# A two-layer encoder step on one core: the first FFN's matmuls in nine orders, the recurrent states in a pool of their own, the residual on another queue

## The chip, the cores and the metric

The kernel runs on one core of one Trainium2 chip. The metric is the device time of one execution in microseconds (us). The core has five engines that run side by side and wait for each other by semaphores: PE (TensorE, matmul), ACT (ScalarE), DVE (VectorE), POOL (GpSimd) and SP (SyncE, which here only issues DMAs). Matmul results land in PSUM, eight banks of 512 fp32 columns on 128 partitions; everything else lives in SBUF.

## The reference

One step of a small streaming encoder, for a prompt of 256 frames and a sample of 32 frames that share all weights; both are handled together as 288 columns. Layer 0 mixes with four retention heads and four gated linear attention (GLA) heads, layer 1 with 16 heads of band attention. Each layer ends in a ConvFFN, and a last RMSNorm gives the output.

```python
def conv_ffn(h, conv_buf, w_up, conv_w, conv_b, w_down):
    up = jnp.einsum('btd,df->btf', h, w_up)          # 2048 -> 2 x 5632
    g, u = jnp.split(up, 2, axis=-1)
    ...
    for w in range(CONV_W):                          # 3 taps along the frames
        gc = gc + gp[:, w:w + T] * conv_w[w]
    act = jax.nn.silu(gc) * u
    return jnp.einsum('btf,fd->btd', act, w_down), gp[:, -(CONV_W - 1):]

def trunk(x, ...):
    for l in range(DEPTH):                           # 2 layers
        h = rmsnorm(x, p['norm_mix_g'][l])
        mix, ... = ab_mixer(h, ...) if l % 2 == 0 else c_mixer(h, ...)
        x = x + mix
        f, buf = conv_ffn(rmsnorm(x, p['norm_ffn_g'][l]), ...)
        x = x + f
    return rmsnorm(x, p['norm_final_g']), ...
```

The states of both kinds of heads are inputs for the sample and outputs for prompt and sample.

## The kernel before

Everything is kept transposed: features on the partitions, the 288 frames along the columns. An fp32 product is made from three products of numbers cut to the PE's fp32r format: a weight tile w (128x128) is split by `weights` into wh (ACT casts, line 62) and wl = w - wh (DVE subtracts, line 63), and an activation into a high half xh and a low half xl that stand side by side in one tile of 576 columns. For each weight tile `both` issues wh times the first 320 columns (line 91: all 288 of xh and 32 of xl) and wh times the other 256 (line 92), and `high` issues wl times xh (line 95, 288 columns). I call these three matmuls a triple. The 32 columns of xl that land at PSUM columns 288 to 319 are added to the front by `joined` on DVE (lines 100 and 101).

`project` makes one 128-wide output: it goes through the input features in chunks of eight weight tiles (512 KB per chunk, one DMA on SP's queue, line 61; four buffers for w, three each for wh and wl), so an input projection is 2 chunks and 16 triples, and a down projection of one half of the FFN is 3 chunks and 22 triples. Its PSUM bank comes from a pool of four (`acc`).

The code is written in the order of the model and a scheduler (the tile framework) turns it into one fixed instruction order per engine; each engine then runs its list strictly in order, and so does each DMA-issuing queue. Where buffers of one pool are reused, or a pool takes the memory of a closed one, the framework puts waits in.

The places that matter below:

- `start`: `first_products` streams the inputs (`xw`: x and the first weights together, 12 DMAs on SP) and multiplies as they land; POOL prepares `lo_h`, the small gate weights. Then comes the product v0, `first_squares` (sum of squares on ACT and DVE), `norm_stat` (line 207: the sum over partitions by a matmul with ones, then 1/sqrt into R), and `second(0)`, the first half of the product v1. The other half is made in the first GLA head, around the gate matmul `first[3]([0])` (line 513), which needs R.
- `gla_head` and `ret_head` load the sample's states into tiles `gst` and `rst` of the mixers' pool `ab` (POOL's queue); at the end of the mixers the new retention states are written out from `rst` (line 832).
- `out_proj`: the pool `x` takes over `ab`'s memory. The residual x is loaded again, in pieces of two feature tiles (lines 294 and on), the first two pieces at once and the others one by one as it goes. After output tile m, DVE adds the product to x[m] (line 304), ACT scales it by the norm's gain (line 184), and the squares are summed.
- `ffn`, for each of two halves of the 5632 features: 22 pairs of input products (g and u), convolution, SiLU and product into the tiles `b`, then 16 down products that are added to x.

## Time and profile before

| what | value |
|---|---|
| median of three runs | 2655.47 us (2654.35 to 2659.1) |
| the profiled execution's own time | 2656.71 us |
| its span, from the first to the last instruction | 2654.9 us |
| PE busy | 2636.5 us, 99% |
| DVE busy / ACT busy / POOL busy | 1708.6 / 1123.6 / 228.9 us (64% / 42% / 9%) |
| mean granted PE clock | 0.997 of full speed |
| bytes moved by DMA | 448.31 MB, mean 169 GB/s |

In the profile a matmul is listed with its line, its output and inputs (buffer numbers left out), the columns, the number of such matmuls and their mean duration. Neighbouring matmuls overlap in the array, so the durations add up to more than the span; the distance from one start to the next is what a matmul costs. A bracket names the idle time ahead of an instruction and who ended it. The clock column gives the share of full speed that the PE was granted.

### The profile page before, as it was taken

The page shows a single profiled execution, that of the slowest core. Times are in us where ns is not written, and L with a number is a line of the kernel's source. Part 1 is how long each engine was busy: PE and PEld are TensorE (multiplying, and loading weights), DVE is VectorE, ACT ScalarE, POOL GpSimd, SP SyncE. Part 2 cuts the span into 40 slices and gives each one's busy share as a digit, 9 for nine tenths or more (in the row PEclk, how much of TensorE's full clock was granted, in tenths as well). Part 3 has the DMA queues.
Part 4 walks back from the last instruction along what each step waited for, and adds up shares of the span by engine and source line. Part 5 has one row for each costly group of instructions (what it writes and reads, how often), then busy time and mean ns, then how long its engine had stood idle before and what let it go on. Part 6 is the DMA issues. An engine that isn't in the chain of part 4 may idle for free.

```text
span 2654.9 us, 49383 instructions
## 1 busy us (share of the span) xinstructions
PE 2636.5 (99%) x20079; PEld 2618.0 (99%) x20079; DVE 1708.6 (64%) x3355; ACT 1123.6 (42%) x1511; POOL 228.9 (9%) x471
## 2 busy tenths in 40 slices
PE   9999999999999999999999999999999999999998
PEld 9999999999999999999999999999999999999997
DVE  8776666677775467776555555567777645777654
ACT  6554444443333333334444344444333333333443
POOL 3000001011110001110021110100111000111000
PEclk9999999999999999999999999999999999999999
DMA  6444555555555555555675565555555555555554
GB/s 231 152 132 160 161 162 168 184 166 167 168 167 162 169 171 168 167 170 163 169 213 181 177 188 167 160 168 165 169 167 170 161 168 173 167 167 168 166 169 132
DMA packets 127584, 448.31 MB, mean 169 GB/s; under 512 B 16155, under 2 KB 16475, under 8 KB 127356
## 3 DMA queue, kind: packets, MB, share of 16 engines
q1 hardware_dynamic: 119564, 424.47, 52.0%
q0 software_dynamic: 7648, 20.65, 2.5%
q8 instruction: 157, 2.57, 0.4%
q14 instruction: 71, 0.58, 0.1%
q10 hardware_dynamic: 144, 0.04, 0.0%
HBM read 434.69 MB, written 10.40 MB: 168 GB/s over the span
## 4 chain that ended last, share of the span: by engine, by line
PE 87%; issue 11%; DMA 0%; DVE 0%; POOL 0%; ACT 0%; DVEq 0%; POOLq 0%; ACTq 0%
PE acc L91 32%; PE acc L95 28%; PE acc L92 25%; PE mm L599 0%; PE mm L913 0%; PE mm L877 0%; DMA x<-in_xT 0%; DMA out_ret_out<-rst 0%; DVE y L370 0%; PE mm L876 0%; PE mm L207 0%; PE mm L914 0%; DMA gains<-in_gains 0%; PE mm L91 0%; PE mm L513 0%
## 5 line engine op out<-in xcount | busy, mean ns | idle before, releaser
L91 PE MATMUL acc<-x,wh 128*128 128x320 f32 x4464 | 1394.9, 313 | 0.3 <-DVE x L185 0.3
L62 ACT CAST wh<-w 128x1024 fp32r<-128x1024 f32 (+1 forms) x812 | 838.8, 1033 | 1288.1 <-PE acc L92 1044.7
L63 DVE TENSOR_TENSOR wl<-w,wh 128x1024 fp32r<-128x1024 f32 (+1 forms) x812 | 977.5, 1204 | 532.8 <-ACT wh L62 521.1
L95 PE MATMUL acc<-x,wl 128*128 128x288 f32 x4464 | 1298.4, 291 | 0.0
L92 PE MATMUL acc<-x,wh 128*128 128x256 f32 x4464 | 1246.5, 279 | 0.0
L91 PEld LDWEIGHTS acc<-x,wh 128*128 128x128 f32 x4464 | 838.4, 188 | 2.3 <-issue 1.1
L92 PEld LDWEIGHTS acc<-x,wh 128*128 128x128 f32 x4464 | 838.5, 188 | 0.8 <-issue 0.3
L95 PEld LDWEIGHTS acc<-x,wl 128*128 128x128 f32 x4464 | 836.9, 188 | 0.1
L91 PE MATMUL acc<-b,wh 128*128 128x320 f32 x1920 | 599.0, 312 | 1.9 <-ACT wh L62 1.9
L95 PE MATMUL acc<-b,wl 128*128 128x288 f32 x1920 | 560.3, 292 | 0.5 <-DVE wl L63 0.5
L92 PE MATMUL acc<-b,wh 128*128 128x256 f32 x1920 | 536.6, 280 | 0.0
L91 PEld LDWEIGHTS acc<-b,wh 128*128 128x128 f32 x1920 | 361.6, 188 | 2.7 <-ACT wh L62 2.4
L95 PEld LDWEIGHTS acc<-b,wl 128*128 128x128 f32 x1920 | 361.4, 188 | 1.1 <-DVE wl L63 0.8
L92 PEld LDWEIGHTS acc<-b,wh 128*128 128x128 f32 x1920 | 361.6, 188 | 0.0
L100 DVE COPY tail<-acc 128x32 f32<-128x32 f32 x376 | 72.0, 192 | 285.7 <-PE acc L95 282.9
L333 POOL COPY conv_out<-gp 128x2 f32<-128x2 f32 x88 | 100.3, 1140 | 1272.5 <-DVE gp L331 1272.5
L161 ACT CAST b<-v 128x288 fp32r<-128x288 f32 x88 | 38.1, 433 | 149.8 <-DVE v L348 149.8
L340 DVE SCALAR_TENSOR_TENSOR gc<-gp,convp,gc 128x290 f32<-128x290 f32 x176 | 91.8, 522 | 6.2
L101 DVE TENSOR_TENSOR acc<-acc,tail 128x32 f32<-128x32 f32 x376 | 74.8, 199 | 12.1
L162 DVE TENSOR_TENSOR b<-v,b 128x288 fp32r<-128x288 f32 x88 | 40.5, 460 | 44.0 <-ACT b L161 44.0
L331 DVE TENSOR_TENSOR gp<-acc,R 128x256 f32<-128x256 f32 x88 | 37.4, 425 | 9.1 <-DVE acc L101 0.5
L346 DVE TENSOR_TENSOR v<-acc,R 128x288 f32<-128x288 f32 x88 | 40.2, 457 | 3.0
(300 smaller groups left out, 1177.9 us busy)
## 6 DMA issues: line engine op xcount, KB each, us to landing
w<-in_w_ffn_up SPq DMA_DIRECT2D x352, 512.0 KB, 3.8
w<-in_w_ffn_down SPq DMA_DIRECT2D x128, 512.0 KB, 3.7
w<-in_w_in SPq DMA_DIRECT2D x108, 512.0 KB, 3.8
w<-in_w_qkv SPq DMA_DIRECT2D x96, 512.0 KB, 3.9
w<-in_w_ffn_down SPq DMA_DIRECT2D x64, 384.0 KB, 3.2
w<-in_w_out_ab SPq DMA_DIRECT2D x32, 512.0 KB, 3.8
w<-in_w_out_att SPq DMA_DIRECT2D x32, 512.0 KB, 3.7
x<-in_xT POOLq DMA_DIRECT2D x8, 288.0 KB, 5.0
```

Source lines behind the costliest of these rows:

```text
L62: nc.scalar.copy(h, w)
L63: nc.vector.tensor_tensor(l, w, h.bitcast(F32), op=ALU.subtract)
L91: nc.tensor.matmul(ps[:, :TX], lhsT=w, rhs=x[:, :TX], start=first, stop=last, skip_group_check=True)
L92: nc.tensor.matmul(ps[:, TX - T : T], lhsT=w, rhs=x[:, TX:], start=False, stop=last, skip_group_check=True)
L95: self.nc.tensor.matmul(ps[:, :T], lhsT=w, rhs=x[:, :T], start=False, stop=last, skip_group_check=True)
L100: self.nc.vector.tensor_copy(x, ps[:, T:TX])
L101: self.nc.vector.tensor_tensor(ps[:, :n], ps[:, :n], x, op=ALU.add)
L161: self.nc.scalar.copy(h, v)
L162: self.nc.vector.tensor_tensor(l, v, h.bitcast(F32), op=ALU.subtract)
L333: nc.gpsimd.tensor_copy(conv_out[:, f, 0:2], gp[:, TP : TP + 2])
L340: nc.vector.scalar_tensor_tensor(gc, gp[:, w : w + W], cw[:, w : w + 1], gc, op0=ALU.mult, op1=ALU.add)
L346: nc.vector.tensor_tensor(v, u, self.R, op=ALU.mult)
```

## The change

1. `project` takes a number `order`. It decides in which sequence the three matmuls of the eight weight tiles of a chunk are issued ("first" is line 91's matmul before, "rest" line 92's, "low" line 95's), and how the 576 columns are divided. All three matmuls per weight tile stay, with 864 columns together. Order 0 is the kernel before. 1: rest, first, low. 2: every other tile backwards. 3: in pairs of tiles. 5: all firsts of the chunk, then all rests, then all lows. 6: first, low, rest. 4: divided 304 + 272 + 288. 8: 288 + 288 + 288, which needs no `joined`. 9: 512 + 64 + 288. 7: the lows collect in a second PSUM bank, which DVE copies and adds at the end.
2. Only layer 0's FFN uses them. Of its first half's input pairs, four each take orders 1, 2, 3, 5 and 6; of its second half's, four each take 4, 7 and 8, and one takes 9; the down products take 1 and 3 in the first half (eight outputs each), 2 and 6 in the second. The other pairs keep order 0.
3. The states get a pool `states` of four tiles that lives through the whole program, outside `ab`: two tiles take the GLA states in pairs and later retention states again.
4. The residual's first two pieces are issued on SP's queue (`nc.sync`) and no longer on POOL's.
5. `norm_stat` of the start is called after `second(0)`, and the first head makes the other half of v1 before the first gate matmul.
6. Some small tiles of the attention's sample part have one buffer where they had two.

```diff
-    def project(self, src, x, nk, k0=0, chunks=None, part=None, ps=None):
+    def project(self, src, x, nk, k0=0, chunks=None, part=None, ps=None, order=0):
...
+        n_first = {4: 304, 8: T, 9: 512}.get(order, TX)
+        lows = self.acc() if order == 7 else ps
...
-            for j in range(n):
+            for step, j in self.steps(order, n, c == chunks[0]):
+                at = x[c + j]
                 first, last = c == chunks[0] and j == 0, c == chunks[-1] and j == n - 1
-                self.both(ps, h[:, j, :], x[c + j], first)
-                self.high(ps, l[:, j, :], x[c + j], last)
+                if step == "low":
+                    self.high(lows, l[:, j, :], at, last, first and order == 7)
+                else:
+                    self.both(ps, h[:, j, :], at, first, last and order == 7, n_first, step)
+        if order == 7:
+            self.nc.vector.tensor_copy(lows[:, T : T + 1], lows[:, :1])
+            low = self.side.tile([P, T], F32, name="lows", tag="lows", bufs=1)
+            self.nc.vector.tensor_copy(low, lows[:, :T])
+            self.nc.vector.tensor_tensor(ps[:, :T], ps[:, :T], low, op=ALU.add)
...
+    def steps(self, order, n, begins):
+        a, b, l = "first", "rest", "low"
+        if order == 3:
+            pairs = [range(j, min(j + 2, n)) for j in range(0, n, 2)]
+            return [(s, j) for p in pairs for s in (a, b, l) for j in p]
+        if order == 5:
+            return [(s, j) for s in (a, b, l) for j in range(n)]
+        of = {1: (b, a, l), 6: (a, l, b)}.get(order, (a, b, l))
+        out = []
+        for j in range(n):
+            turned = order == 2 and j % 2 == 1
+            mine = (a,) + tuple(s for s in of if s != a) if begins and j == 0 else (l, b, a) if turned else of
+            out += [(s, j) for s in mine]
+        return out
...
+        self.stp = ctx.enter_context(self.tc.tile_pool(name="states", bufs=GRP))
...
-        self.norm_stat()
         v1 = self.mm()
         second = lambda part: self.project(w[VB + 1], self.xx, KD, chunks=(0, WCH), part=part, ps=v1)
         second(0)
+        self.norm_stat()
...
-            piece(0, 2)
-            piece(2, 2)
+            piece(0, 2, nc.sync)
+            piece(2, 2, nc.sync)
...
+        of = ((1, 2, 3, 5, 6), (4, 7, 8, 9))[half]
+        at = f // 4
+        n = 1 if at < len(of) and of[at] == 9 else 4
+        return of[at] if layer == 0 and at < len(of) and f % 4 < n else 0
...
+        v1 = first[4](1) if first else self.input_product(w[VB + 2 * hd + 1])
         if first:
             first[3]([0])
-        v1 = first[4](1) if first else self.input_product(w[VB + 2 * hd + 1])
...
-        st = pool.tile([P, 256], F32, name="gst", tag="gst", bufs=GRP)
-        nc.gpsimd.dma_start(st, a["state_gla"][hd])
-        sts.append(st)
+        if hd % 2 == 0:
+            st = self.stp.tile([P, 512], F32, name="st", tag="st")
+            sts += [st[:, :256], st[:, 256:]]
+        nc.gpsimd.dma_start(sts[hd], a["state_gla"][hd])
```

How this moves instructions is seen in three places. At the head of the program, POOL before had only the gate weights to prepare (`lo_h` from the landed `xw`):

```order
L274 MEMSET lo_h 128x16x96
L131 CAST lo_h<-xw 128x16
L132 ISA
L132 TENSOR_TENSOR lo_h<-xw,lo_h 128x16
L131 CAST lo_h<-xw 128x16 x7
L132 TENSOR_TENSOR lo_h<-xw,lo_h 128x16 x7
L131 CAST lo_h<-xw 128x2x16
```

Now the state tiles `st` depend on nothing, and on POOL their loads stand there too:

```order
L308 MEMSET lo_h 128x16x96
L611 DMA st<-in_state_gla 128x256 x3
L163 CAST lo_h<-xw 128x16
L611 DMA st<-in_state_gla 128x256
L164 ISA
L164 TENSOR_TENSOR lo_h<-xw,lo_h 128x16
L163 CAST lo_h<-xw 128x16 x7
L163 CAST lo_h<-xw 128x2x16
L164 TENSOR_TENSOR lo_h<-xw,lo_h 128x16 x7
L781 DMA st<-in_state_ret 128x512
```

Six state loads have moved from the mixers to the first instructions of POOL's list, and the cast of the ninth and tenth gate tiles has gone ahead of seven subtractions.

At the start's norm, this is DVE's list before, from the low weights of the next product to the gate input `lo`:

```order
L63 TENSOR_TENSOR wl<-w,wh 128x1024
L505 MEMSET lo 33x288
L171 TENSOR_SCALAR rv<-mm 128x288
L173 TENSOR_TENSOR rs<-rs,rv 128x288
L174 SCALAR_TENSOR_TENSOR R<-rs,ry 128x288
L506 TENSOR_TENSOR lo<-acc,R 32x288
```

And this is DVE's list there after:

```order
L63 TENSOR_TENSOR wl<-w,wh 128x1024
L547 MEMSET lo 33x288
L63 TENSOR_TENSOR wl<-w,wh 128x1024
L203 TENSOR_SCALAR rv<-mm 128x288
L205 TENSOR_TENSOR rs<-rs,rv 128x288
L206 SCALAR_TENSOR_TENSOR R<-rs,ry 128x288
L132 COPY tail<-mm 128x32
L548 TENSOR_TENSOR lo<-acc,R 32x288
```

One more subtraction of weights now stands ahead of the norm's first step (its cast has moved ahead of the norm on ACT likewise), and the tail of v1 ahead of `lo`.

At the output projection, POOL before had the first residual pieces right behind the retention states' stores:

```order
L788 DMA out_ret_out<-so 128x512 x2
L832 DMA out_ret_out<-rst 128x512 x4
L294 DMA x<-in_xT 128x576 x2
L548 DMA convp<-in_convp 128x176
L548 DMA hist<-in_hist 128x88
```

SP's list after has them among the weights of the output projection:

```order
L61 DMA w<-in_w_in 128x1024 x108
L61 DMA w<-in_w_out_ab 128x1024 x10
L328 DMA x<-in_xT 128x576 x2
L61 DMA w<-in_w_out_ab 128x1024 x22
L61 DMA w<-in_w_ffn_up 128x1024 x88
```

The two pieces have left POOL's list and stand behind the tenth chunk of output weights, and what they wait for is no longer the stores of the states, whose tiles lie outside the memory that x takes.

More of the change, by code (lines that the diff above doesn't have):

```diff
@@ L94, in high @@
[L94 to L101 removed]
+        if step != "rest":
+            nc.tensor.matmul(ps[:, :n], lhsT=w, rhs=x[:, :n], start=first, stop=last, skip_group_check=True)
@@ L354, in ffn @@
             for m in range(KD):
[L355 removed]
+                ps = self.project(down[m], bb, HALF, half * HALF, order=((1, 3), (2, 6))[half][m // 8] if layer == 0 else 0)
                 nc.vector.tensor_tensor(self.x[m], self.x[m], ps, op=ALU.add)
```

57 lines of the change are left out of this document (31 added, 26 removed).

## The prediction

> **What bounds the kernel now.** I read the page's busy times first, then the waits of PE, then the order in time around each wait.
>
> ```profile
> span 2654.9 us, 49383 instructions
> PE 2636.5 (99%) x20079; PEld 2618.0 (99%) x20079; DVE 1708.6 (64%) x3355; ACT 1123.6 (42%) x1511; POOL 228.9 (9%) x471
> ```
>
> PE is the bound from end to end, so the time changes in two ways only: a triple gets dearer or cheaper, or PE idles more or less. The waits of PE say where it idles:
>
> ```profile
> PE mm L207 <- issue: 1.9, 1, 1.9
> PE acc L91 <- ACT wh L62: 1.9, 1, 1.9
> PE acc L95 <- DVE wl L63: 0.5, 1, 0.5
> ```
>
> The first is the start's norm, the other two belong to the output projection of layer 0. The table of stretches gives the price of a triple where nothing is waited for, in layer 0's FFN (columns: stretch, length, then PE, PEld, DVE, ACT, POOL busy with their instructions, clock, DMA):
>
> ```profile
> 600.00:800.00 200.00, 200.00 (x1528) 200.00 (x1527) 141.26 (x269) 77.61 (x95) 24.94 (x48) 1.00 0.54 168
> ```
>
> 1528 matmuls in 200 us are 0.131 us each, 0.3927 us per triple. DVE is busy for 71% there, ACT for 39%; neither holds PE up.
>
> **The residual on SP's queue, its memory free of the states.** PE's order in time at the output projection:
>
> ```profile
> 453.29 0.31 PE L91 MATMUL acc<-b,wh 128*128 128x320 f32 x1
> ...
> 455.75 0.55 PE L91 MATMUL acc<-b,wh 128*128 128x320 f32 x1 [1.90 <-ACT wh L62]
> 456.09 0.42 PE L92 MATMUL acc<-b,wh 128*128 128x256 f32 x1
> 457.00 0.61 PE L95 MATMUL acc<-b,wl 128*128 128x288 f32 x1 [0.50 <-DVE wl L63]
> 457.41 0.47 PE L91 MATMUL acc<-b,wh 128*128 128x320 f32 x1
> ...
> 458.13 0.47 PE L91 MATMUL acc<-b,wh 128*128 128x320 f32 x1
> ...
> 462.97 0.31 PE L91 MATMUL acc<-b,wh 128*128 128x320 f32 x1
> ```
>
> and the stretches beside it:
>
> ```profile
> 458.00:460.00 2.00, 2.00 (x10) 2.00 (x10) 1.93 (x5) 0.69 (x2) 0.00 (x0) 0.50 0.79 267
> 464.00:466.00 2.00, 2.00 (x18) 2.00 (x17) 0.89 (x2) 0.17 (x1) 0.00 (x0) 1.00 1.03 387
> ```
>
> From 453.29 to 462.97 PE does ten triples in 9.68 us; at 0.3927 they take 3.93, so 5.75 us are lost here. Only 3.3 of them are waits (two triples from 453.29 to 457.41, 4.12 us less 0.79); in the rest the granted clock is 0.50 and a triple takes 0.72 us. The reader sees that a wait of PE costs more than itself. Why did ACT come late with its weights? The chain of waits (start, length, what):
>
> ```profile
> 441.74 4.27 DMA out_ret_out<-rst
> 446.79 0.53 POOL x L294
> 447.32 5.75 DMA x<-in_xT
> ```
>
> and ACT's order in time:
>
> ```profile
> 444.32 1.05 ACT L62 CAST wh<-w 128x1024 fp32r<-128x1024 f32 x1 [2.06 <-PE acc L92]
> 453.13 0.54 ACT L184 ACTIVATE x<-x,gains 128x288 fp32r<-128x288 f32 x1 [7.76 <-DMA x<-in_xT]
> 454.66 1.03 ACT L62 CAST wh<-w 128x1024 fp32r<-128x1024 f32 x1
> ```
>
> POOL holds the residual's DMA until the states are stored out of the memory it will fill; ACT, strictly in order, waits 7.76 us for it, and the next cast of weights stands behind. After the change the load waits for SP's tenth chunk of output weights instead:
>
> ```profile
> 439.08 0.33 SPq L61 DMA_DIRECT2D w<-in_w_out_ab  x1
> ```
>
> which lands about 4.5 us after its issue (the DMA issues of that stretch):
>
> ```profile
> w<-in_w_out_ab SPq DMA_DIRECT2D x3, 512.0 KB, 4.5
> ```
>
> It is issued at about 439.5 and, beside the stores and two weight chunks, lands by 444 to 446, which is when ACT has finished its last early cast. ACT then has some 7 us in hand against 453.13. Queued behind it on SP is the eleventh chunk, whose buffer has to come free first, so the wait of 0.4 us or so holds nothing up. I take the whole 5.75 us as a gain; below it is bounded by nothing more to save, above by no gain at all if the load still waits. What is late next: nothing within 7 us on ACT, so the cover is thick.
>
> By the Trainium skill, page "TensorE: Matmul & The Clock Gate", Part 1, the clock halves only after an idle window of about 3.4 us; by that rule the idle times here (1.9 and 0.5 us) would not have halved it, the gain would be 3.3 us and the sum below 2.4 us higher. The trace shows the half clock after them, and the trace decides.
>
> **The states in their own pool.** Four GLA loads of 128 KB now go out at once on POOL, in the stretch from 2 to 14 us in which the start's input stream runs. DMA queues and issues there (the last two lines are those of the first 40 us):
>
> ```profile
> DMA packets 1883, 4.59 MB, mean 382 GB/s; under 512 B 329, under 2 KB 363, under 8 KB 1883
> q1 hardware_dynamic: 1739, 4.54, 99.9%
> xw<-in_x_first SPq DMA_DIRECT2D x8, 280.0 KB, 4.3
> gst<-in_state_gla POOLq DMA_DIRECT2D x4, 128.0 KB, 3.2
> ```
>
> The 16 DMA engines are full (99.9%), and one feature tile of 280 KB takes 0.75 us at 382 GB/s. PE needs 0.79 us for it (two outputs, two triples each 0.395 us, below), so it follows the stream with almost no slack. 524 KB more at 382 GB/s are 1.37 us; I take +1.3 us, between 0 (the added loads yield) and 1.7 (the gate subtractions on POOL that now wait for a later landing hold PE up too). The two retention loads come when PE is 1.7 us behind the stream or more: nothing.
>
> **The start's norm behind second(0).** PE, ACT and DVE in order of time:
>
> ```profile
> 28.34 0.29 PE L95 MATMUL acc<-x,wl 128*128 128x288 f32 x1
> 30.54 0.72 PE L207 MATMUL mm<-xw,ones 128*128 128x288 f32 x2 [1.91 <-issue]
> 31.30 0.50 ACT L170 ACTIVATE ry<-mm,ones 128x288 f32<-128x288 f32 x1 [1.72 <-PE mm L207]
> 34.92 0.29 PE L95 MATMUL mm<-x,wl 128*128 128x288 f32 x1
> 35.22 0.72 PE L513 MATMUL mm<-lo,w 33*128 33x288 f32 x2
> 43.39 2.35 DVE L63 TENSOR_TENSOR wl<-w,wh 128x1024 fp32r<-128x1024 f32 x2
> 44.63 0.31 PE L91 MATMUL acc<-x,wh 128*128 128x320 f32 x1
> ```
>
> The 1.91 us in front of L207, and 0.17 more before L513 (0.30 from start to start where 0.13 is usual), vanish. But from the norm's first step on ACT to the gate matmul L513 it takes 3.92 us (31.30 to 35.22), which before lay beside v1's products. Now ACT has one more cast ahead of that step, whose buffer is free only when PE has done second(0). Worked through with the start 1.3 us later: second(0) ends at 32.95, cast and norm step begin at 34.05, the gate matmul could run at about 38.1; PE is through with v1 at 36.7 and waits 1.4 us. Behind the gate the chain goes on to the low weights of the second gate product, which before were ready at 44.6 (43.39 plus half of 2.35) for a product that began at 44.63: no slack. The shifted chain delivers them about 0.9 us late. So 2.1 us are saved and 2.3 come back: +0.2, with ends of -1.2 (ACT's cast does no harm) and +1.0.
>
> **The orders.** 1760 triples change: 33 pairs of 32 triples and 32 down products of 22. The trace holds one other neighbourhood, the first products, where two outputs alternate, with a low after a low and a bank change:
>
> ```profile
> 21.14 0.30 PE L91 MATMUL acc<-x,wh 128*128 128x320 f32 x1
> ...
> 21.66 0.43 PE L95 MATMUL acc<-x,wl 128*128 128x288 f32 x2
> 21.93 0.30 PE L91 MATMUL acc<-x,lo_h 128*128 128x320 f32 x1
> ```
>
> Two triples in 0.79 us, 0.395 each: 2.3 ns above the steady ones. If all 1760 paid that, it is +4.0 us; nothing excludes as much gain, so the ends are -4 and +4. I take 0: the columns stay 864, each of the three still loads its own weights, and the neighbourhood hardly matters.
>
> Order 9 is priced apart: its 64-column matmul must also load 128x128 weights. The nearest row is that of the GLA scores, with 64 columns and new weights for each:
>
> ```profile
> 51.36 0.89 PE L599 MATMUL mm<-qk 128*128 128x64 f32 x7
> L599 PE MATMUL mm<-qk 128*128 128x64 f32 x112 | 14.6, 265 | 0.0
> ```
>
> Seven starts in 0.89 us less one duration of 0.265 are 0.104 us apart, while in proportion to 0.3927 us for 864 columns 64 would cost 0.029 to 0.036. That is 0.07 us for each of 32 triples: +2.2 us, with ends 0 and +2.6.
>
> Order 7 adds three DVE instructions per product, about 1.07 us by the row of a 288-column PSUM operation, 0.46 us, for two of them:
>
> ```profile
> L346 DVE TENSOR_TENSOR v<-acc,R 128x288 f32<-128x288 f32 x88 | 40.2, 457 | 3.0
> ```
>
> A pair lasts 12.6 us, in which DVE is busy for 8.9 (71%) and then 11.0 us. Both chunks of the next product are already split when these instructions begin, so PE has 6.3 us of cover; the fourth bank is freed about 3.3 us after g ends and needed after 6.3. Without that cover PE would wait some 3 us per pair. Cost: 0. Order 8's missing joins and the single attention buffers cost and bring nothing, DVE not being waited for there.
>
> **Sum.** -5.75 + 1.3 + 0.2 + 0 + 2.2 = -2.05 us against the profiled execution's 2656.71 us, that is 2654.7. The median shown is 2655.47, 1.2 below that execution, so I predict 2653.4 for the median. About 0.2% (5.3 us) is what a measurement of this kernel tells from no change.
>
> **Rivals.**
> - The residual still comes late. Its wait list also holds older DMAs of POOL and PE's last state matmuls; if one lands after 448, ACT blocks as before. The sum is then +3.7: 2659.2 us. Against it stand the 7 us of slack. Chance 0.08. The Trainium skill, page "Trainium Kernel Development and Optimization", section "Key Constraints", says that all queues run on the same 16 DMA engines and another queue only saves issue time; by this rule the move by itself brings nothing, and the gain rests on the changed wait alone.
> - The orders cost more than the first products show (slower). Every changed neighbourhood pays 5 ns per triple: 1760 x 5 ns = 8.8 us, 2662.2 us. It decides for slower from 4.2 ns (7.4 us over 1760). For it: the alternating triples are dearer by 2.3 ns. Chance 0.10.
> - Order 7 makes PE wait for a bank, 3.2 us for each of four pairs, 13 us: 2666 us. Chance 0.04.
> - The orders gain: 4 ns per triple, for instance because the same weights are no longer loaded twice running (orders 5 and 6) or the 320-column matmul (313 ns against 291 for 288) loses its surcharge. -7 us, 2646.4 us. Chance 0.12.
> - The early state loads cost nothing at the start: 2651.9 us. Chance 0.16.
>
> **Numbers.** The forecast, 2653.4, has a chance of 0.50. Faster by over 0.2% (below 2650.2): most of the gaining orders, a third of the free loads, a little of the forecast: 0.20. Slower (above 2660.8): most of the dear orders, order 7, some of the late residual and the forecast's edge: 0.15. Within: 0.65. The range 2647 to 2661 leaves out about 0.18: half of the gaining and most of the dear orders, and order 7.
>
> **What would show it.** Right: near 450 us no wait of ACT's gain for the residual, clock 1.00 throughout, triples of 0.39 us; in the first 12 us feature tiles that start over 0.79 us apart; a PE wait of 1 to 2 us at the gate matmul in place of that at L207, and another of about 1 us at the second gate product; 0.39 us per triple in all orders but 9, and about 0.46 in 9. Wrong: a half clock in the output projection, PE waits in the second half's input pairs four to seven, or triples that differ by 4 ns or more from 0.3927.

## The result: 0.25% slower

| | before | changed |
|---|---|---|
| median of 7 runs each, us | 2655.47 (2654.35 to 2659.14) | 2663.63 (2662.03 to 2664.81) |
| ratio, 95% interval | 1 | 1.0025 [1.0015, 1.0035] |
| profiled execution, us | 2656.71 | 2663.31 |
| its span, mean granted clock | 2654.9, 0.997 | 2661.5, 0.998 |

The forecast was 2653.4 us, with 2647 to 2661 as range; the time lies above both. The medians differ by 8.2 us (the interval goes from 4.0 to 9.3), the two profiled executions by 6.6; the account below is that of the profiled executions. The page of the changed kernel opens with these lines:

```profile
span 2661.5 us, 49416 instructions
PE 2644.4 (99%) x20079; PEld 2624.4 (99%) x20079; DVE 1711.4 (64%) x3363; ACT 1124.7 (42%) x1511; POOL 217.8 (8%) x469
```

PE is the bound as before, with as many matmuls, and its busy time grew by 7.9 us (2636.5 to 2644.4). So the loss is not a new wait: matmuls take longer. The waits of PE after the change (us in total, times, longest):

```profile
PE mm L555 <- issue: 1.1, 1, 1.1
PE acc L123 <- DVE wl L63: 1.1, 1, 1.1
PE acc L118 <- DVE x L217: 0.6, 2, 0.3
```

The 1.9 us for the late cast and the 1.9 us at the start's norm are gone; there is a wait at the gate matmul (now L555), one at low weights, and two at the first products, of which the kernel before had one (0.3 us). PE's list has the same number of matmuls in both kernels, so the starts of matmuls at the same place of the list can be subtracted. Cut at fixed places, that gives the whole account (us from one place to the next):

| stretch of PE's work | before | changed | difference | forecast |
|---|---|---|---|---|
| first products, first to 65th matmul | 8.68 | 10.68 | +2.00 | +1.3 |
| from there to behind the second gate product, with the norm | 34.51 | 34.88 | +0.37 | +0.2 |
| rest of the mixer, but for its last 37 us | 352.47 | 352.43 | -0.04 | 0 |
| these 37 us and the output projection of layer 0 | 137.44 | 131.72 | -5.72 | -5.75 |
| layer 0's FFN: order 9 | | | +2.57 | +2.2 |
| layer 0's FFN: the other orders | | | +7.05 | 0 |
| (FFN in all) | 831.41 | 841.03 | +9.62 | +2.2 |
| from there to the last matmul | 1273.46 | 1273.44 | -0.02 | 0 |
| sum | | | +6.2 | -2.05 |

**The output projection** went as forecast. SP's queue, ACT's order in time and two stretches of the changed kernel; the last row is the first of these stretches in the kernel before:

```profile
442.14 0.80 SPq L328 DMA_DIRECT2D x<-in_xT  x2
...
448.26 0.54 ACT L216 ACTIVATE x<-x,gains 128x288 fp32r<-128x288 f32 x1 [3.62 <-DVE x L338]
```

```profile
454.00:456.00 2.00, 2.00 (x18) 2.00 (x17) 2.00 (x5) 1.22 (x2) 0.54 (x1) 1.00 0.88 304
458.00:460.00 2.00, 2.00 (x18) 2.00 (x17) 1.36 (x4) 0.92 (x2) 0.54 (x1) 1.00 0.97 322
454.00:456.00 2.00, 0.26 (x1) 0.26 (x2) 1.95 (x7) 1.95 (x4) 0.77 (x4) 0.97 0.00 0
```

The residual is issued at 442.14, ACT's first gain no longer waits for a DMA, PE has 18 matmuls in each 2 us where it had 1 and 10 (the 10 stand in the prediction's rows), and the clock is 1.00.

**The orders.** The table of stretches, changed kernel; in this sequence: order 6, old order, order 3, order 8, order 7.

```profile
736.00:786.00 50.00, 50.00 (x377) 50.00 (x376) 34.98 (x67) 18.85 (x23) 6.23 (x12) 1.00 0.51 166
786.00:811.00 25.00, 25.00 (x193) 25.00 (x192) 17.62 (x34) 9.90 (x12) 3.07 (x6) 1.00 0.54 162
884.00:944.00 60.00, 60.00 (x456) 60.00 (x455) 28.05 (x42) 20.51 (x21) 0.00 (x0) 1.00 0.56 167
1054.00:1102.00 48.00, 48.00 (x365) 48.00 (x364) 31.58 (x55) 18.99 (x24) 1.96 (x12) 1.00 0.52 168
1004.00:1052.00 48.00, 48.00 (x368) 48.00 (x368) 40.02 (x85) 18.25 (x22) 1.78 (x11) 1.00 0.52 170
```

And the kernel before in the first and third of these stretches:

```profile
736.00:786.00 50.00, 50.00 (x384) 50.00 (x383) 35.23 (x69) 19.66 (x24) 6.23 (x12) 1.00 0.54 166
884.00:944.00 60.00, 60.00 (x460) 60.00 (x459) 28.80 (x42) 20.58 (x21) 0.00 (x0) 1.00 0.58 167
```

PE is busy all the time, at full clock, and gets 7 matmuls fewer through in 50 us, 4 fewer in 60. Nothing waits; the triples are dearer. From the start of the first triple of each group to the start of the next group, in ns per triple (393.3 in the kernel before; the first 128 of order 1, where the layer's norm lies between, are left out):

| order | 1, 6 | 2, 3, 8 | 4 | 5 | 7 | 9 |
|---|---|---|---|---|---|---|
| ns per triple | 399.3 to 400.0 | 396.7 | 397.8 | 394.1 | 393.4 | 473.5 |

Order 9 in PE's order of time:

```profile
1110.06 0.39 PE L118 MATMUL acc<-x,wh 128*128 128x512 f32 x1
1110.29 0.19 PE L120 MATMUL acc<-x,wh 128*128 128x64 f32 x1
1110.32 0.38 PE L123 MATMUL acc<-x,wl 128*128 128x288 f32 x1
1110.53 0.39 PE L118 MATMUL acc<-x,wh 128*128 128x512 f32 x1
```

From 512 to 512 it takes 0.47 us. The low product seems to start 0.03 us behind the 64 columns, but its follower starts 0.21 us later where 0.13 is usual: the missing time stands in the row behind the short matmul.

### The profile page after: what moved, and what is told of

Read it like the earlier page. It is cut to its first block, busy times and chain, and to the rows that moved or that the text cites. A ratio compares the mean times of both kernels' runs of the same rounds, so it can differ in the third digit from the quotient of the medians.

```text
span 2661.5 us, 49416 instructions
## 1 busy us (share of the span) xinstructions
PE 2644.4 (99%) x20079; PEld 2624.4 (99%) x20079; DVE 1711.4 (64%) x3363; ACT 1124.7 (42%) x1511; POOL 217.8 (8%) x469
## 3 DMA queue, kind: packets, MB, share of 16 engines
q8 instruction: 157, 2.57, 0.4%
## 4 chain that ended last, share of the span: by engine, by line
PE 98%; DVE 1%; ACT 0%; DMA 0%; issue 0%; SPq 0%; DVEq 0%
PE acc L118 35%; PE acc L123 31%; PE acc L120 28%; PE mm L642 0%; PE mm L956 0%; PE mm L920 0%; DMA xw<-in_x_first 0%; PE mm L460 0%; PE mm L829 0%; PE mm L708 0%; DVE y L412 0%; PE mm L919 0%; PE mm L671 0%; ACT wh L62 0%; PE mm L442 0%
## 5 line engine op out<-in xcount | busy, mean ns | idle before, releaser
L118 PE MATMUL acc<-x,wh 128*128 128x320 f32 (+2 forms) x4464 | 1354.9, 312 | 0.7 <-DVE x L217 0.6
L123 PE MATMUL acc<-x,wl 128*128 128x288 f32 x4464 | 1266.5, 293 | 1.1 <-DVE wl L63 1.1
L120 PE MATMUL acc<-x,wh 128*128 128x256 f32 (+2 forms) x4464 | 1219.0, 280 | 0.0
L118 PEld LDWEIGHTS acc<-x,wh 128*128 128x128 f32 x4464 | 827.0, 188 | 3.5 <-issue 1.5
L120 PEld LDWEIGHTS acc<-x,wh 128*128 128x128 f32 x4464 | 829.5, 188 | 0.8 <-issue 0.3
L118 PE MATMUL acc<-b,wh 128*128 128x320 f32 x1920 | 568.2, 311 | 0.0
L123 PE MATMUL acc<-b,wl 128*128 128x288 f32 x1920 | 533.6, 293 | 0.0
L120 PEld LDWEIGHTS acc<-b,wh 128*128 128x128 f32 x1920 | 357.8, 188 | 0.0
L118 PEld LDWEIGHTS acc<-b,wh 128*128 128x128 f32 x1920 | 350.5, 188 | 0.6 <-ACT wh L62 0.3
L132 DVE COPY tail<-acc 128x32 f32<-128x32 f32 (+1 forms) x366 | 69.7, 191 | 273.5 <-PE acc L123 258.7
L375 POOL COPY conv_out<-gp 128x2 f32<-128x2 f32 x88 | 76.6, 871 | 1282.0 <-DVE gp L373 1282.0
L133 DVE TENSOR_TENSOR acc<-acc,tail 128x32 f32<-128x32 f32 (+1 forms) x366 | 72.6, 198 | 11.5
```

Of the source, the lines that this page charges most:

```text
L118: nc.tensor.matmul(ps[:, :n], lhsT=w, rhs=x[:, :n], start=first, stop=last, skip_group_check=True)
L120: nc.tensor.matmul(ps[:, n - T : T], lhsT=w, rhs=x[:, n:], start=False, stop=last, skip_group_check=True)
L123: self.nc.tensor.matmul(ps[:, :T], lhsT=w, rhs=x[:, :T], start=first, stop=last, skip_group_check=True)
L132: self.nc.vector.tensor_copy(x, ps[:, T:end])
L133: self.nc.vector.tensor_tensor(ps[:, :n], ps[:, :n], x, op=ALU.add)
L375: nc.gpsimd.tensor_copy(conv_out[:, f, 0:2], gp[:, TP : TP + 2])
```

## The experiments

Each ratio is to the kernel before on the same chip, with its 95% interval.

**Apart: the orders, and all the rest.** Two runs split the change in two. In the first, every product goes back to the old order:

```diff
-        return of[at] if layer == 0 and at < len(of) and f % 4 < n else 0
+        return 0
...
-                ps = self.project(down[m], bb, HALF, half * HALF, order=((1, 3), (2, 6))[half][m // 8] if layer == 0 else 0)
+                ps = self.project(down[m], bb, HALF, half * HALF, order=0)
```

> The changed kernel with every product in the old order (first, rest, low; 320 and 256 columns, no order 9, no lows of their own), everything else as changed. Theory (the orders cost, the rest is as the two traces show): the FFN of layer 0 takes 831.4 us again instead of 841.0, so the run is 9.6 us below the changed kernel, 2654.0, and 1.5 us below the kernel before... worked from the shifts of the two traces: -5.72 at the output projection, +2.36 at the start, so -3.4 against before: 2652.1 us. Rival (the FFN is slower because of the other allocation of memory, not for its orders): FFN still near 840 us, total 2661 to 2663.

In the second, the orders stay, and the states, the residual's queue and the norm are as before. The first gate's new place and the single small buffers stay too:

```diff
+        self.norm_stat()
...
         second(0)
-        self.norm_stat()
...
-            piece(0, 2, nc.sync)
-            piece(2, 2, nc.sync)
+            piece(0, 2)
+            piece(2, 2)
...
+        st = pool.tile([P, 256], F32, name="gst", tag="gst", bufs=GRP)
+        nc.gpsimd.dma_start(st, a["state_gla"][hd])
...
-        st = self.stp.tile([P, 512], F32, name="st", tag="st")
...
+        st = pool.tile([P, 2, 256], F32, name="rst", tag="rst", bufs=GRP)
+        nc.gpsimd.dma_start(st, a["state_ret"][hd])
```

> The kernel before with the orders alone: states in the mixer's pool, the residual on POOL's queue, the norm behind v0 as before. Theory: +9.6 us in layer 0's FFN and nothing elsewhere, 2665.1 us; triples of 399 to 401 ns in orders 1 and 6, 396.7 in 2 and 3, 401 in 8, 454 in 9. Rival (the price comes from where the tiles lie in memory, so it goes with the states' pool): triples at 393.3 in all orders but 9, and 2657 us.

Measured: 2653.72 us, 0.9985 [0.9976, 0.9994], for the old orders; 2667.25 us, 1.0037 [1.0024, 1.0049], for the orders alone. Layer 0's FFN takes 831.41 us in the one and 841.02 in the other, to 0.01 us what it takes before and after the change. The expectation of the second missed two prices: order 8 takes 396.7 ns there, not 401, and order 9 473.5, not 454 (the next expectation uses this 454 again). The stretch of order 6, orders alone:

```profile
736.00:786.00 50.00, 50.00 (x378) 50.00 (x377) 34.19 (x67) 18.51 (x22) 6.75 (x12) 1.00 0.48 159
```

So the orders carry the whole loss, 9.6 us, in either layout of the memory, and without them the change would be a gain. The rival of the other allocation falls.

**What in an order costs.** A menu varies one thing at a time in the triples of the input products, 64 triples of a kind. An entry holds the weights (h: the high ones in all three), the sequence of first, rest and low (0, 1, 2), and for each its first column, its columns and its PSUM column:

```diff
+ MENU = [('', (0, 1, 2), [(0, 320, 0), (320, 256, 32), (0, 288, 0)]),
+  ('', (0, 2, 1), [(0, 320, 0), (320, 256, 32), (0, 288, 0)]),
+  ('h', (0, 1, 2), [(0, 320, 0), (320, 256, 32), (0, 288, 0)]),
...
+  nc.tensor.matmul(out[:, po : po + n_], lhsT=(l if s == 2 and key != "h" else h)[:, j, :], rhs=at[:, xo : xo + n_], ...)
```

> A menu for measuring, not a version: layer 0's input products take 22 kinds of triple in turn, two feature blocks (64 triples) each, all else as in the changed kernel with the old order; the products of that layer are not those of the reference, since columns, weights and places in PSUM are varied. Pairs of kinds hold the cycles first-rest-low (393 ns in the changed kernel) and first-low-rest (400 ns) against each other. Theory (the price hangs on the sizes of neighbouring matmuls alone): the 7 ns between the two cycles stay when all three take the same weights, when rest writes from PSUM column 0, when rest reads the high columns, and with all of these. Rivals: it hangs on the weights (7 ns vanish with the same weights thrice), on the PSUM columns (vanish with rest from column 0, or with low from column 32), on the columns read (vanish with rest from the high columns). For the division: 352/224, 384/192, 416/160, 448/128, 480/96 and 512/64 cost 393 as long as the smaller one covers the weight load of its follower, and from there on 0.42 ns per column less: by 453.6 ns at 64 the edge would lie near 200 columns. Three matmuls of 128 columns each then show the weight load itself: about 95 to 125 ns a piece, 285 to 375 ns per triple; three of 256 about 345.

Measured, in ns per triple from the starts of the records (trimmed mean of 56):

| | first, rest, low | first, low, rest |
|---|---|---|
| as in the kernel | 393.3 | 400.0 |
| high weights in all three | 393.3 | 400.0 |
| rest into PSUM column 0 | 393.3 | 400.0 |
| rest reads the high columns | 393.3 | 400.0 |
| all of these | 393.3 | 400.0 |
| low reads from column 32 | 400.6 | 398.1 |

The table of stretches shows it too; in this sequence: first-low-rest and first-rest-low of the same weights, then three of 256, and three of 128 columns:

```profile
558.00:582.00 24.00, 24.00 (x182) 24.00 (x181) 17.18 (x32) 9.29 (x12) 2.05 (x6) 1.00 0.52 173
583.50:607.50 24.00, 24.00 (x186) 24.00 (x185) 17.29 (x32) 9.50 (x12) 3.13 (x6) 1.00 0.52 174
951.00:971.00 20.00, 20.00 (x175) 20.00 (x174) 15.10 (x29) 8.45 (x11) 3.08 (x6) 1.00 0.59 191
995.00:1015.00 20.00, 20.00 (x180) 20.00 (x179) 16.50 (x34) 8.28 (x12) 3.12 (x6) 1.00 0.61 197
```

(The first of the four takes the low weights for its low product, the second the high ones; the rows of the table say that this changes nothing.) So the 7 ns between the cycles hang on the numbers of columns and their sequence; weights, PSUM columns and the place that rest reads fall as rivals. The last row is an exception: it was said of PSUM, but in this kind low reads from column 32, and that moves both. Three of 128 columns take 335 ns, three of 192 as well, 112 each, so that is a floor; three of 256 take 347, three of 288 400. The divisions 352/224, 384/192, 416/160, 448/128, 480/96 and 512/64 take 406, 421, 434, 448, 460 and 473 ns, 13.4 more for each 32 columns. This part of the expectation was wrong: it had put the edge near 200 columns, and the price rises at once beyond 320/256. A shorter rest saves nothing, since below 256 columns its place is held by the 112 ns, while the longer first costs its columns in full.

**How smooth it is.** The second menu takes 44 kinds: divisions with n columns in the first, the same in the other cycle (first, low, rest), and equal or mixed sizes. An entry now holds, for each matmul in its sequence, the weights, the first column read, the columns and the PSUM column:

```diff
+MENU = [[('h', 0, 288, 0), ('h', 288, 288, 0), ('l', 0, 288, 0)],
+ [('h', 0, 296, 0), ('h', 296, 280, 8), ('l', 0, 288, 0)],
...
+ [('h', 0, 296, 0), ('l', 0, 288, 0), ('h', 296, 280, 8)],
...
+ [('h', 0, 256, 0), ('h', 0, 256, 0), ('h', 0, 256, 0)],
...
```

> A second menu for measuring, not a version: the input products of both layers take 44 kinds of triple in turn, 64 triples each, so they are not those of the reference; all else as in the changed kernel with the old order. From the first menu: three of 288 take 400 ns, three of 256 345, three of 192 or 128 334 (111 each, the bound of the weight load), and only the sizes count. Theory A (each matmul takes the longer of 111 ns and its columns at 2.4 GHz plus 13.3 ns, less some ns for a matmul under about 272 columns): the divisions in the order first, rest, low fall from 400 at 288/288 to a lowest value at about 320/256 and rise by 0.42 ns per column beyond; the reversed cycle stays near 400 from 296 to 320 and meets it beyond 328. Theory B (320/256 is a point by itself, for instance since 256 columns are a whole number of something): 316, 318, 322 and 324 columns stand several ns above 320. Three equal matmuls of 256, 260, 264, 268, 272, 280 columns show which: a smooth rise (A) or a step behind 256 (B).

| columns of the first | 288 | 300 | 304 | 308 | 312 | 316 | 318 | 320 | 322 | 324 | 326 | 332 | 336 |
|---|---|---|---|---|---|---|---|---|---|---|---|---|---|
| ns per triple | 397 | 396 | 398 | 400 | 395 | 399 | 397 | 393 | 394 | 397 | 400 | 395 | 397 |

Three equal matmuls of 256, 260, 264, 268, 272, 280 and 296 columns take 347, 360, 361, 376, 370, 387 and 420. Neither theory holds as it stood: there is no smooth curve (268 columns cost more than 272, 296 more than the 416 of 304) and 320/256 isn't alone by itself, only the lowest of a rugged row; all lie between 393 and 401. The seven divisions tried in the other cycle take 395 to 400. The stretches of 312/264, 314/262 and 320/256:

```profile
660.00:684.00 24.00, 24.00 (x185) 24.00 (x184) 17.42 (x34) 9.61 (x12) 3.12 (x6) 1.00 0.51 174
686.00:710.00 24.00, 24.00 (x183) 24.00 (x182) 16.97 (x32) 9.17 (x12) 3.12 (x6) 1.00 0.49 169
762.00:786.00 24.00, 24.00 (x186) 24.00 (x185) 17.48 (x33) 9.41 (x12) 3.12 (x6) 1.00 0.49 174
```

No division or cycle tried beats the old one.

**Where a matmul reads.** The last menu shifts the first column that each matmul reads, all into PSUM column 0 with the high weights:

```diff
+MENU = [[('h', 0, 320, 0), ('h', 0, 256, 0), ('h', 0, 288, 0)],
+ [('h', 0, 320, 0), ('h', 0, 256, 0), ('h', 16, 288, 0)],
...
+ [('h', 16, 320, 0), ('h', 0, 256, 0), ('h', 0, 288, 0)],
...
+ [('h', 0, 320, 0), ('h', 16, 288, 0), ('h', 0, 256, 0)],
...
+ [('h', 0, 304, 0), ('h', 0, 272, 0), ('h', 0, 288, 0)],
...
+ [('h', 0, 304, 0), ('h', 304, 272, 0), ('h', 0, 288, 0)],
...
```

> A fourth menu for measuring, not a version: the input products of both layers take 44 kinds of triple, all with the high weights and into PSUM column 0, so they are not those of the reference; what varies is the column at which a matmul starts to read, beside a few sizes. What the menus before left open: reading the low columns from 32 instead of 0 moved 393.3 to 400.6 and 400.0 to 398.1, and three of 288 took 397 where the second read from column 288 and 400 where all read from 0. Theory A (reads that start off a multiple of 64 columns, 256 bytes, are dearer or shift the rhythm): starts at 64, 128 and 320 leave 393.3 as it is, starts at 16, 32, 48, 288 and 304 move it by 2 to 7 ns, and the divisions 304, 308, 312, 316, 324 and 332, read from 0 in all three, lie on a smooth line between 393 and 400. Theory B (it is a matter of lengths and phases alone, and the start of a read only shifts the phase): starts at 64 or 128 move it as much as those at 32, and the divisions read from 0 stay as rugged as before, 395 to 400 without order.

| ns per triple of 320, 256, 288 | 0 | 16 | 32 | 48 | 64 | 96 | 128 |
|---|---|---|---|---|---|---|---|
| low (288) reads from | 393.4 | 396.6 | 401.9 | 397.8 | 393.3 | 400.6 | 393.3 |
| first (320) reads from | | 399.7 | 393.3 | | 393.3 | | 393.3 |
| rest (256) reads from | | 395.5 | 393.3 | | 393.3 | | 393.3 |

The stretches of low from 32, low from 64, and of 304/272/288 read from 0 and with rest from column 304 (the kernel's order 4):

```profile
584.00:608.00 24.00, 24.00 (x182) 24.00 (x181) 16.98 (x32) 9.50 (x12) 3.13 (x6) 1.00 0.52 173
635.00:659.00 24.00, 24.00 (x186) 24.00 (x185) 17.41 (x33) 9.66 (x12) 3.13 (x6) 1.00 0.52 175
2014.50:2038.50 24.00, 24.00 (x185) 24.00 (x184) 17.24 (x32) 9.46 (x12) 3.13 (x6) 1.00 0.51 174
2065.00:2089.00 24.00, 24.00 (x183) 24.00 (x182) 17.10 (x32) 9.33 (x12) 3.14 (x6) 1.00 0.55 169
```

Half of theory A holds: starts at a multiple of 64 columns leave the price as it is, in every kind where they were tried, and in this cheap cycle a start at 16 raises it; at 32 it depends on the matmul. But off a multiple of 64 the price doesn't only rise. In the other cycle, 320, 288, 256, it falls from 400.0 to 393.5 when the 288 columns are read from 16, and three of 288 fall from 399.7 to 395.7 when the second is read from 16. Such a start is therefore not dear by itself: in what was tried it left or raised the price of the cheap sequence and lowered that of the dear ones. Order 4's division costs 393.3 when all three read from 0, so its 4.4 ns are the place that rest reads. The other half of theory A is wrong: 308, 316, 324 and 332 columns, all read from 0, still take 400, 400, 397 and 400. And three of 256 take 340 and 353 ns in turn from product to product; what alternates with the products was not varied. The last nanoseconds thus hang also on the column at which a read starts, which the order of instructions alone doesn't tell.

**Is it the weight load?** The third menu keeps the sizes and shrinks the weights:

```diff
+MENU = [(128, 128, 320, 256, 288),
+ (128, 128, 320, 288, 256),
+ (128, 64, 320, 256, 288),
...
+                    self.nc.tensor.matmul(ps[:cols, :n_], lhsT=h[:rows, j, :cols],
+                                     rhs=at[:rows, :n_], start=False, stop=last and last_s,
+                                     skip_group_check=True)
...
```

> A third menu for measuring, not a version: layer 0's input products in 22 kinds of triple, all from PSUM column 0 with the high weights, with fewer weight columns (64, 32) or fewer weight rows (64, 32) than 128; the products are not those of the reference. Theory A (the odd 7 ns of an order come from how the weight load lies beside the matmul ahead of it): with 64 or 32 weight columns or rows the load is shorter, three matmuls of 128 columns fall from 334 towards 200 ns, and the two cycles of 320, 256 and 288 columns come out alike. Theory B (they come from the columns streamed and their lengths, whatever the weights): 393 and 400 stay in every form, and 334 for three of 128 may fall or not. The last rows hold three of 64 columns (load bound: 334 again by A and B), and 512/64/288 with 64 weight columns, 473 ns if the bound is the load of any weights, nearer 400 if a load of half the columns takes half.

| weights, rows x columns | 320, 256, 288 | 320, 288, 256 | 3 of 288 | 3 of 128 | 512, 64, 288 |
|---|---|---|---|---|---|
| 128 x 128 | 393.3 | 400.0 | 400.0 | 335 (first menu) | 473 (first menu) |
| 128 x 64 | 395.0 | 393.2 | 395.1 | 180 | 415 |
| 128 x 32 | 393.2 | 393.0 | 390.0 | 180 | |
| 64 x 128 | 393.8 | 400.0 | 400.1 | | |

In this sequence: first-low-rest with 128 and with 64 weight columns, three of 128 with 64 weight columns (PE is busy for 11.99 of 15 us there, being ahead of DVE), 512/64/288 with 64 (415 is the price of three of its four products; in the first the clock was still half):

```profile
560.00:584.00 24.00, 24.00 (x183) 24.00 (x182) 17.08 (x32) 9.38 (x12) 2.06 (x6) 1.00 0.52 173
611.00:635.00 24.00, 24.00 (x185) 23.34 (x184) 17.02 (x32) 9.25 (x12) 3.13 (x6) 1.00 0.51 172
661.00:676.00 15.00, 11.99 (x179) 11.52 (x178) 12.96 (x27) 7.92 (x10) 1.52 (x3) 1.00 0.59 200
1283.00:1308.00 25.00, 25.00 (x179) 19.48 (x178) 14.81 (x29) 8.47 (x10) 2.94 (x5) 0.98 0.45 148
```

Theory A holds for the columns of the weights and not for their rows: with fewer weight columns the two cycles come out alike, the floor falls from 112 to at most 60 ns, and order 9's division loses 58 of its 80 ns; with half the rows nothing changes. So the 6.7 ns between the two cycles and most of order 9's price go with the columns of the weights. The load of the next weights, which goes on beside the matmul ahead of it, fits this: 256 columns hide it just so, 64 do not. Two things stay open. Fewer weight columns also mean fewer rows written to PSUM, and that was not tried apart. And no run shows why one sequence of the same sizes, or one start of a read, costs more than another when the weights have 128 columns in both. The Trainium skill, page "TensorE: Matmul & The Clock Gate", section "LDWEIGHTS (loading the stationary operand)", gives the load as the weights' columns divided by 1.2 ns, 107 ns for 128, whatever the rows; the runs agree to 5% with their 112, and in that 64 rows take as long as 128.

**Where the start's 2 us come from.** One run puts the norm back ahead of second(0), with the old orders:

```diff
+        self.norm_stat()
...
         v1 = self.mm()
...
         second(0)
-        self.norm_stat()
```

> As the run with the old order everywhere, and the start's norm back in its old place ahead of second(0). Theory by the prediction's step (the moved norm saves 2.1 us and gives 2.3 to 2.4 back): within 0.3 us of that run, 2651.8 us, with a wait of about 1.9 us at the norm's matmul and none at the gate. Rival (the move of the norm carries most of the 2.36 us at the start): 2650 us or less. Rival (the start's waits for late tiles had given the norm's chain its cover, and putting it back brings the old 1.9 us on top): 2654 us.

A second one also holds the state loads back until the norm is known:

```diff
+        nc.vector.tensor_copy(sts[hd][:, :1], self.R[:, :1])
         nc.gpsimd.dma_start(sts[hd], a["state_gla"][hd])
...
+        nc.vector.tensor_copy(st[:, :1], self.R[:, :1])
         nc.gpsimd.dma_start(st.rearrange("p (j v) -> p j v", j=2), a["state_ret"][hd])
```

> The run with the old order and the old place of the norm, and now each state load waits for a one-column copy of the norm's result on DVE, so that it goes out after 31 us instead of at 2 us. Theory (the early loads take the start's DMA engines from the input stream, 2.1 to 2.4 us): the first 15 us run as in the kernel before, the output projection keeps its 5.7 us, so 2.2 us less than that run, and -5.7 us (ratio 0.9979) against the kernel before on the same chip. Rival (the start is late for another cause, such as the lower clock of the first triples): no change against that run, ratio 0.9988. Rival (with the loads back at 34 us POOL's queue is late for something else): above it.

Measured: 2653.78 us, 0.9989 [0.998, 0.9998], and 2651.97 us, 0.9984 [0.9975, 0.9992]. These intervals overlap, so the whole times don't tell the two apart; the stretches of the traces do. The first is like the run with the norm moved (0.9985); in the traces the stretch with norm and gate takes 34.5 us with the norm ahead and 34.9 behind, so moving it costs 0.4 us. The first products take 10.91 us in the first and 9.09 in the second. Over all traces of versions they take 10.68 to 11.17 us in the four with early loads (mean 10.96) and 8.68 to 9.52 in the five without (mean 9.16): 1.8 us, so the theory's 2.1 to 2.4 were a little high, and the rival that the loads are not the cause falls. The rival of a lower clock in the first triples can be looked at too. In the changed kernel's trace a matmul of 256 columns takes 0.21 us there from its start to the next, where it takes 0.12 in the trace before (changed first), though the clock column gives 1.00:

```profile
5.59 0.41 PE L120 MATMUL acc<-x,wh 128*128 128x256 f32 x1
5.80 0.47 PE L118 MATMUL acc<-x,wh 128*128 128x320 f32 x1
```

```profile
5.46 0.28 PE L92 MATMUL acc<-x,wh 128*128 128x256 f32 x1
5.58 0.30 PE L91 MATMUL acc<-x,wh 128*128 128x320 f32 x1
```

The first eight matmuls take 2.08 us at this half pace, 1.22 before. It isn't the cause: the changed kernel in the old orders takes 1.17 us for them and still 11.17 for the first products, since PE then waits for the tiles instead. But it is part of the scatter among the traces without early loads. The changed kernel at the start, a wait of PE for the next tile, and the DMA queues and issues from 2 to 14 us:

```profile
9.00 0.39 PE L118 MATMUL acc<-x,wh 128*128 128x320 f32 x1 [0.25 <-DVE x L217]
```

```profile
q1 hardware_dynamic: 1577, 4.04, 88.3%
q0 software_dynamic: 192, 0.52, 12.2%
st<-in_state_gla POOLq DMA_DIRECT2D x4, 128.0 KB, 5.5
```

The states take 12.2% of the 16 engines there, 1.5 of the 12 us, and the inputs' share falls from 99.9 to 88.3%. With the states late, the inputs have 100.2% again:

```profile
q1 hardware_dynamic: 1674, 4.46, 100.2%
```

A small part of the 1.8 us, 0.1 to 0.5 us by the traces with early loads, goes through POOL instead. At the end of this stretch the gate matmuls follow POOL's subtractions, which now stand behind the cast of the ninth and tenth gate tiles: in the run with the old orders the eighth subtraction ends at 15.85 us and its matmul starts at 15.90. The prediction's upper end had allowed for this.

**Queue or memory.** The residual moved to another queue, and its memory lost the states. One run undoes the first alone, the other (from the kernel before) does the first alone:

```diff
-            piece(0, 2, nc.sync)
-            piece(2, 2, nc.sync)
+            piece(0, 2)
+            piece(2, 2)
```

> The run with the old order and the old place of the norm, with the residual's first two pieces on POOL's queue again; states stay in a pool of their own. Theory (the residual was late because its memory held the states until their stores had landed, not because of the queue): POOL issues the load without waiting for a store to land, ACT does not wait for it, and the 5.7 us stay gained: the same as that run, ratio 0.9988, clock 1.00 from 454 to 466 us. Rival (the queue is what matters): POOL's order puts it behind the four stores, ACT waits again, some 4 to 5.7 us come back, ratio 1.0005 to 1.001.

```diff
-            piece(0, 2)
-            piece(2, 2)
+            piece(0, 2, nc.sync)
+            piece(2, 2, nc.sync)
```

> The kernel before with one edit: the residual's first two pieces go out on SP's queue; states stay in the mixer's pool. Theory (the memory decides): SP now waits for the states' stores to land (to about 446 us), and the two weight chunks behind it wait too; the residual still lands at 450 to 452, PE still stalls, and the stall is as long or longer by the late weights: 0 to +3 us against the kernel before. Rival (the queue alone brings the gain): -5.7 us, ratio 0.9979.

Measured: 2655.54 us, 0.9997 [0.9988, 1.0006], with the memory alone; 2653.45 us, 0.9988 [0.9979, 0.9997], with the queue alone. The first also has the start's early loads and, in its trace, 1.57 us of half clock at the norm, so I go by the stretch of the output projection as cut above: 137.44 us before, 133.43 with the memory alone, 132.45 with the queue alone, 131.72 with both. The run with the orders alone has the old code there and takes 136.19, with a shorter half clock; the stall thus costs 4.5 to 5.7 us, the memory alone saves 2.8 to 4.0 of it and the queue alone 3.7 to 5.0. The chain of waits of the two, memory alone first:

```profile
446.43 0.53 POOL x L328
446.96 6.20 DMA x<-in_xT
```

```profile
442.65 4.08 DMA out_ret_out<-rst
446.93 3.21 DMA x<-in_xT
```

Both theories were too simple. With free memory POOL still issues the load behind its four stores, only without waiting for them to land, and it takes 6.2 us. On SP it still waits for a store to land, as said, but then needs 3.21 us, not 5.75, and PE's wait there is 0.5 us in all. Why it lands sooner there wasn't tried by itself and stays open. Either part takes most of the stall, also because the shorter waits (0.4 and 0.7 us with the memory alone) were not followed by the half clock in these two traces, memory alone first:

```profile
458.00:460.00 2.00, 2.00 (x17) 2.00 (x16) 2.00 (x5) 2.00 (x4) 0.54 (x1) 1.00 0.95 303
```

```profile
458.00:460.00 2.00, 2.00 (x17) 2.00 (x17) 1.93 (x5) 0.84 (x3) 0.00 (x0) 1.00 0.96 367
```

The two parts together take all of it.

**Cover for the gate.** The last run moves the first gates' matmul behind the next product, with the norm moved, states late and old orders:

```diff
-        if first:
-            first[3]([0])
...
         z = [gate(0)] if first else []
+        if first:
+            first[3]([0])
```

> The run with the states loaded late, with the norm behind second(0) as in the change, and one more move: the first gates' matmul goes behind the whole next product on PE (6.3 us of work) instead of in front of it. Theory (the moved norm saves its 2.1 us, and 2.4 come back because the chain from the norm to the gate, 3.9 us, has lost its cover): now the gate is covered too, from the norm to the third matmul behind the second gate product no wait of 1 us is left, and the run is 2 us below the one with the states late, 2650.0 us, ratio 0.9976 to its kernel before. Rival (DVE's later work, above all the scan of the gates that stands in its row, only moves the wait on to the low weights of another product): the 1.1 us wait at low weights stays, and 0.5 to 1 us at most are gained, ratio 0.998. Rival (the first GLA head now waits for its later sums): no gain, ratio 0.9984.

Measured: 2651.27 us, 0.9979 [0.997, 0.9988]. The stretch with norm and gate takes 33.72 us, where it takes 34.44 with the states late alone: 0.7 us, which is what the first rival gave (0.5 to 1), though not for its reason. The gate's wait is gone, that at the low weights too, and another one stands ahead of the next product:

```profile
37.38 0.39 PE L118 MATMUL acc<-x,wh 128*128 128x320 f32 x1 [1.18 <-DVE lo L548]
```

The product needs a PSUM bank that still holds the gate's input until DVE has multiplied it by the norm. So the norm's result has a second user that PE waits for. This version beats the kernel before by 0.2% and the changed one by 0.5%, the best of the runs; the interval of the run with the states late overlaps with it.

## Why the prediction failed, step by step

- **The orders (forecast 0, measured +7.05 us): the step that failed.** It said "the columns stay 864, each of the three still loads its own weights, and the neighbourhood hardly matters". The runs showed that the sequence of the three matmuls, their division and the column at which rest reads cost up to 6.7 ns per triple, 4.1 on the mean of 1728 triples, with PE busy throughout and wherever the states and the residual lie. The price is uneven: orders 1 and 6 carry about 3.8 of the 7.05 us, order 7 nothing. The ends of the term, -4 and +4 us, were too narrow as well: they came from the one other neighbourhood in the trace, 2.3 ns dearer per triple, and a single row doesn't bound eight other sequences. Of the rivals "the orders cost more" (5 ns per triple, 2662.2 us) came nearest, at a chance of 0.10, and the prediction's own sign of being wrong, triples that differ by 4 ns or more, is there in orders 1, 4 and 6, and on the edge in 2, 3 and 8. The row that spoke for it was there, the first products. I set the price to 0 because it could also have gone the other way; the steady 0.3927 us of one good cycle was no reason for that.
- **Order 9 (forecast +2.2, measured +2.57, end +2.6): right.** The row of the 64-column scores gave 0.104 us for a matmul with new weights; the floor measured here is 0.112.
- **The residual (forecast -5.75, measured -5.72): right in the mechanism, with some luck in the number.** The half clock is gone with the wait, but the same old code lost 1.25 us less in the run with the orders alone, and against that run the gain is 4.5 us. The prediction's sentence that the move to another queue by itself brings nothing did not hold: alone it brought 3.7 to 5.0 us.
- **The state loads (forecast +1.3, measured +2.00, +1.8 over all traces): right in kind, just outside the upper end of 1.7.** The 1.37 us were bytes by rate; in the trace the packets held the engines for 12.2% of 12 us, 1.46 us. The trace of before (8.68) was the shortest of the five without early loads; the means of the two groups differ by 1.8 us. The rival of free loads should read 2652.1 us by the prediction's own terms (2653.4 less 1.3), not 2651.9.
- **The norm (forecast +0.2, measured +0.37): right**, with the waits of 1.1 us at the gate and 1.1 us at the second gate product where 1.4 and 0.9 were said.
- **Order 7 and order 8's joins (forecast 0): right.** 393.4 ns in order 7 with DVE busy for 40.02 of 48 us; 396.7 in order 8 is the price of its division read as in the kernel (397 in the menu).
- **The sum.** With the orders' 7.05 us and the 0.7 us that the start's term lacked it would have been +5.7, within 0.5 us of the account. The other 2 us by which the medians lie apart are within what runs of the same kernel differ by (4.8 us between the lowest and the highest of the kernel before).

## What to carry to other kernels

On an engine that is busy 99% of the time, an order of instructions isn't free until a row shows that very order: where a neighbouring order in the trace already costs 0.6% more, forecast a loss and a range wider than that one row. Keep matmuls long enough to hide the load of the next weights (here 256 columns for 128 weight columns), and when you divide columns unevenly, count the short one at no less than that load. Measure a sequence together with the columns at which it reads: here starts at a multiple of 64 columns changed nothing, and others moved a triple by up to 8.5 ns, up or down. Loads that nobody needs yet should not be freed to start while the input stream fills the DMA engines: one wait on a late result got 1.8 us back.

## What the runs showed of the hardware beside that

A wait of the same length may or may not be followed by the half clock. The norm's wait at the start is 1.9 us in both of these runs with the same code ahead of it; the first is the one with the norm back, the second that with the residual on POOL:

```profile
35.00:37.00 2.00, 2.00 (x17) 2.00 (x17) 0.88 (x2) 1.32 (x4) 2.00 (x7) 1.00 0.83 257
```

```profile
35.00:37.00 2.00, 2.00 (x10) 2.00 (x10) 0.85 (x2) 1.08 (x3) 2.00 (x8) 0.50 0.81 242
```

The second lost 1.57 us by it (36.05 against 34.48 us for the stretch with norm and gate), which has nothing to do with its edit. The Trainium skill, page "TensorE: Matmul & The Clock Gate", Part 1, calls the window in which idle time is counted free-running, which fits that difference; its 3.4 us of idle time do not fit a half clock behind 1.9 us.

The clock also fell with PE busy throughout: in the third menu, triples of 320, 256 and 288 columns with 32 weight rows ran at half clock, 720 ns each, though PE had no idle time. The clock had fallen at about 994 us, in the kind before them (64 weight rows, three of 128 columns), and came back at about 1284, with 128 weight rows again since 1217:

```profile
1030.00:1076.00 46.00, 46.00 (x186) 44.49 (x185) 15.93 (x29) 8.50 (x11) 3.11 (x6) 0.50 0.27 91
```
